# Modulation loads in buffers of their own, table loads and padding behind the first h, and half-contraction first feed-forward rounds in a hybrid decoder layer

## The chip, the cores and the metric

The kernel runs on 1 core of one Trainium2 chip. The metric is the device time of one execution in microseconds; three runs of the kernel before have a median of 1298.05 us (1289.34 to 1298.52).

## The reference

One decoder layer on x (256 tokens, 2048 features, float32), with a conditioning vector c. Six modulation vectors of 2048 come out of c; attention (8 heads) and a state-space branch (S5 and a gated linear unit) share one input and one output projection; a squared-ReLU feed-forward of 8192 follows.

```python
mod = (jax.nn.silu(c) @ w_ada + b_ada)[:, None, :]
sh1, sc1, g1, sh2, sc2, g2 = jnp.split(mod, N_MOD, axis=-1)

h = rms_norm(x, norm1_g) * (1.0 + sc1) + sh1
proj = h @ w_in
q, k, v, u = jnp.split(proj, [ATTN_WIDTH, 2 * ATTN_WIDTH, 3 * ATTN_WIDTH], axis=-1)
q = rms_norm(q.reshape(bsz, s, N_HEADS, HEAD_DIM), q_norm_g)
k = rms_norm(k.reshape(bsz, s, N_HEADS, HEAD_DIM), k_norm_g)
attn = dilated_attention(q, k, v).reshape(bsz, s, ATTN_WIDTH)

y = jax.nn.gelu(s5_mixer(u, lam_re, lam_im, log_step, b_re, b_im, c_re, c_im, d_skip))
ssm = y * jax.nn.sigmoid(y @ w_glu + b_glu)
mixed = jnp.concatenate([rms_norm(attn, attn_out_g), rms_norm(ssm, ssm_out_g)], axis=-1) @ w_out
x = x + g1 * mixed

h2 = rms_norm(x, norm2_g) * (1.0 + sc2) + sh2
ff = jnp.square(jax.nn.relu(h2 @ w_ff1)) @ w_ff2
return x + g2 * ff
```

## The kernel before, in words

**Products.** Activations lie feature-major, 256 tokens in the free dimension. Every large product is made of three reduced-precision products: a float32 value is split into a rounded part and a rest (`split`: ScalarE copies the rounded part, line 161, VectorE subtracts, line 136), for weights (`wh`, `wl`) and activations alike, and TensorE adds high by high, high by low and low by high. All weights come from memory in loads of 512 KB into `raw`, a pool of five buffers, and each is split once.

**Modulation.** `w_ada` is 96 MB in 24 blocks of four "pieces" of 1 MB. Blocks in PE_BLOCKS (8 of them) are multiplied on TensorE against a padded c (`cpad`, line 249, 2 to 4 short matmuls a load), the others on VectorE, which multiplies and sums along the row against a broadcast c (`cbc`, line 158, one instruction of 1024 columns per 512 KB). `pump(n)` takes the next n pieces, in the order ADA_ORDER; `pump_at(i)` takes PUMPS[i] of one. Where a piece is loaded is `ring["tags"]`, set from RINGS by stage: `raw`, the same pool as the weights (two halves of 512 KB), or a buffer that is unused just then (U, T0, PD, WB0). The first `h` group needs 8 pieces, the second 16, the third 24, the fourth 32; the output projection 48; the group kg of `h2`, the input of the feed-forward, 56 + 8 kg; the last ones are due at the end.

**Stages.** After c is padded and the tables of the state-space branch are loaded (`bb`, `cc`, `ident`), `make_h(0..3)` makes the normalised input in four groups of 512 features. The input projection (lines 193 to 195) interleaves with that, block by block over its 8 blocks of 512 output columns, u first; it is evicted into U, V and QK. Between its blocks stand the preparation of the state-space tables (`pad_write`, `toep_half`: copies on ScalarE, small matmuls), the state (`state_in`) and its scan, VectorE steps over the state H in XT. Then come the norms of q and k, `y_block` (lines 686 and 690, 32 steps of small matmuls on the finished state), the gate of the linear unit (`w_glu`, lines 798 to 800), attention in four pairs of heads, and `branch_scale`, which norms a branch and splits it. The output projection takes the state-space half first (8 `w_out_pair` of two 512 KB loads, called pairs of rounds here), then the attention half. `make_h2` and the feed-forward follow: 128 loads for `ff1`, 128 for `ff2`.

**A pair.** `pair_part` takes one 512 KB load of weights, makes 8 matmuls of 512 columns (line 848: the split activation's two parts side by side) and 8 of 256 (line 850) into two accumulator banks; the two halves of a bank are added on the way out. A pair works through 16 matmuls this way.

**Order.** The framework's scheduler decides at build how each engine's instructions are ordered, and every engine then works in that order. SyncE (SP) issues all loads, so a load that waits for its buffer holds up those behind it.

## Time and profile before

| | |
|---|---|
| median of three runs | 1298.05 us |
| profiled execution | 1299.06 us, of which span 1297.3 |
| mean granted TensorE clock | 0.946 of full |
| TensorE busy | 1198.6 us (92%), 6818 matmuls |
| VectorE busy | 921.8 us (71%) |
| ScalarE busy | 582.0 us (45%) |
| moved by DMA | 299.59 MB, 231 GB/s |

Engines: PE is TensorE's matmuls, PEld its weight loads, DVE VectorE, ACT ScalarE, SP SyncE. L848 is line 848 of the kernel before. An instruction is written output<-inputs, with a width, and a bracket behind it says how long its engine stood idle just before and what released it. The clock is a share of the full 2.4 GHz. Matmul durations overlap, so the distance from one start to the next is what a matmul costs in a full queue.

### The profile page before, as it was taken

How to read it: one execution, taken by the hardware profiler on the slowest of the kernel's cores; microseconds unless marked ns; L12 is line 12 of the kernel's file. 1: busy time of each engine (PE TensorE's matmuls, PEld its weight loads, DVE VectorE, ACT ScalarE, POOL GpSimd, SP SyncE). 2: the span in 40 equal slices, each digit the busy share in tenths (PEclk: the TensorE clock that was granted, in tenths of full speed). 3: DMA queues.
4: the chain of work that ended last, by engine and by line, in shares of the span. 5: the costliest groups of instructions: out<-in, count | busy, mean ns of one | idle time of the engine just before them, and what ended most of it. 6: DMA issues, size and time to landing. Idle time of an engine off the chain costs nothing.

```text
span 1297.3 us, 17972 instructions
## 1 busy us (share of the span) xinstructions
PE 1198.6 (92%) x6818; PEld 993.7 (77%) x6818; DVE 921.8 (71%) x1520; ACT 582.0 (45%) x807; POOL 13.0 (1%) x12
## 2 busy tenths in 40 slices
PE   5777999998987977949999999999999999999998
PEld 1355778865677866838888888888888888888887
DVE  9687678899555898877865556765566666667764
ACT  3579544322275533324544444443344443344432
POOL 3000000000000000000000000000000000000000
PEclk9788999999688897969999999999999999999999
DMA  9687898888544486748766666765677666667763
GB/s 345 228 271 259 337 341 314 286 313 289 196 149 162 149 302 213 255 154 275 242 220 188 189 217 224 248 192 184 190 233 239 224 183 191 205 235 248 241 211 96
DMA packets 82166, 299.59 MB, mean 231 GB/s; under 512 B 9120, under 2 KB 11424, under 8 KB 80288
## 3 DMA queue, kind: packets, MB, share of 16 engines
q1 hardware_dynamic: 82080, 298.45, 69.2%
q8 instruction: 53, 0.87, 0.3%
q14 instruction: 33, 0.27, 0.1%
HBM read 296.31 MB, written 2.10 MB: 230 GB/s over the span
## 4 chain that ended last, share of the span: by engine, by line
PE 76%; DVE 8%; DMA 7%; ACT 6%; issue 2%; SPq 0%; DVEq 0%; ACTq 0%
PE acc L848 37%; PE acc L850 18%; DMA raw<-w_ada 6%; PE acc L194 4%; PE acc L195 4%; PE acc L193 4%; DVE wl L136 2%; PE tr L249 2%; DVE raw L158 2%; PE acc L690 1%; ACT wh L161 1%; PE tr L553 1%; PE acc L686 1%; ACT TO L161 1%; PE tr L848 1%
## 5 line engine op out<-in xcount | busy, mean ns | idle before, releaser
L136 DVE TENSOR_TENSOR wl<-raw,wh 128x1024 fp32r<-128x1024 f32 x360 | 439.8, 1223 | 260.6 <-ACT wh L161 259.6
L161 ACT ACTIVATE wh<-raw 128x1024 fp32r<-128x1024 f32 x360 | 381.3, 1060 | 505.5 <-PE acc L848 347.2
L158 DVE SCALAR_TENSOR_TENSOR raw<-raw,cbc 128x1024 f32<-128x1024 f32 x112 | 136.6, 1222 | 53.7 <-DMA raw<-w_ada 53.1
L848 PE MATMUL acc<-CA,wh 128*128 128x512 f32 x608 | 167.0, 397 | 2.5 <-DVE XT L156 2.0
L848 PE MATMUL acc<-TO,wh 128*128 128x512 f32 x480 | 132.0, 396 | 0.6 <-DVE rows L136 0.6
L848 PE MATMUL acc<-QK,wh 128*128 128x512 f32 x384 | 107.4, 402 | 13.1 <-DVE QK L136 13.1
L848 PEld LDWEIGHTS acc<-CA,wh 128*128 128x128 f32 x608 | 104.7, 189 | 16.7 <-issue 2.2
L850 PEld LDWEIGHTS acc<-CA,wl 128*128 128x128 f32 x608 | 92.4, 188 | 13.1
L850 PE MATMUL acc<-CA,wl 128*128 128x256 f32 x608 | 96.1, 281 | 0.0
L848 PEld LDWEIGHTS acc<-TO,wh 128*128 128x128 f32 x480 | 82.5, 189 | 11.7 <-PE acc L850 0.8
L848 PEld LDWEIGHTS acc<-QK,wh 128*128 128x128 f32 x384 | 67.4, 193 | 22.4 <-issue 13.3
L850 PEld LDWEIGHTS acc<-TO,wl 128*128 128x128 f32 x480 | 73.3, 188 | 10.6
L850 PE MATMUL acc<-TO,wl 128*128 128x256 f32 x480 | 76.1, 281 | 0.0
L848 PE MATMUL acc<-WB,wh 128*128 128x512 f32 x256 | 69.8, 394 | 0.0
L850 PEld LDWEIGHTS acc<-QK,wl 128*128 128x128 f32 x384 | 58.3, 189 | 7.7
L850 PE MATMUL acc<-QK,wl 128*128 128x256 f32 x384 | 60.3, 279 | 0.0
L193 PE MATMUL acc<-wh,HA 128*128 128x512 f32 x128 | 48.6, 411 | 9.0 <-ACT wh L161 8.9
L194 PE MATMUL acc<-wl,HA 128*128 128x512 f32 x128 | 52.2, 408 | 0.0
L194 PE MATMUL acc<-wl,HB 128*128 128x512 f32 x128 | 50.7, 397 | 0.4 <-DVE wl L136 0.4
L195 PE MATMUL acc<-wh,HA 128*128 128x512 f32 x128 | 50.6, 401 | 0.0
L195 PE MATMUL acc<-wh,HB 128*128 128x512 f32 x128 | 50.0, 393 | 0.0
L848 PEld LDWEIGHTS acc<-WB,wh 128*128 128x128 f32 x256 | 43.7, 188 | 5.6
(269 smaller groups left out, 1763.5 us busy)
## 6 DMA issues: line engine op xcount, KB each, us to landing
raw<-w_ff SPq DMA_DIRECT2D x256, 512.0 KB, 4.3
raw<-w_ada SPq DMA_DIRECT2D x158, 512.0 KB, 5.2
raw<-w_in SPq DMA_DIRECT2D x64, 512.0 KB, 5.9
raw<-w_out SPq DMA_DIRECT2D x32, 512.0 KB, 4.8
U<-w_ada SPq DMA_DIRECT2D x8, 1024.0 KB, 7.3
XT<-xT SPq DMA_DIRECT2D x8, 512.0 KB, 5.8
T<-w_ada SPq DMA_DIRECT2D x8, 512.0 KB, 6.5
raw<-w_glu SPq DMA_DIRECT2D x8, 512.0 KB, 6.0
```

What stands on the lines that cost most here:

```text
L136: return (eng or self.nc.vector).tensor_tensor(out, a, b, op=op)
L158: self.nc.vector.scalar_tensor_tensor(out, a, s, b, op0=op0, op1=op1, accum_out=accum)
L161: self.nc.scalar.activation(out, a, AF.Copy, scale=scale)
L193: mm(ps, xh, wh, start=start, stop=False)
L194: mm(ps, xh, wl, start=False, stop=False)
L195: mm(ps, xl, wh, start=False, stop=stop)
L249: mm(acc[32 * q : 32 * q + 32, :], cpad[:, 4 * g + q, :], raw[:, i, :], start=g == 0, stop=g == 3,)
L553: mm(pv[:, r - r2, ri], wb[r // 8][:, r % 8, ri], u2[:, :, r, :], start=True, stop=True)
L686: mm(pv[:, r - r8], toep[:, r].rearrange("p g s j -> p (g s j)"), u2[:, :, r, :], start=True, stop=False)
L690: mm(pv[pr, r - r8], ca[pr, r, ri].rearrange("p s j -> p (s j)"), H[pr, ri, r, :], start=False, stop=ri == 1,)
L848: mm(pp[e], hi[:, e, kk], xs[kk].rearrange("p s n -> p (s n)"), start=first and kk == 0, stop=False)
L850: mm(pp[e][:, 0:SEQ], lo[:, e, kk], xs[kk][:, 0], start=False, stop=last and kk == 3)
```

## The change

**Loads.** RINGS and PUMPS change. The first pieces go to three buffers of 1 MB (Q, K, U; `QK` becomes two tensors, Q and K), in one load each, then Q and K alternate; `raw` and the old mixed rings come in the middle; from the norm of q and k on, pieces go to HA alone, from the gate on to HA and PD, one load of 1 MB each; from the feed-forward on to `raw`. The loads of `bb` and `cc` come after five pieces, `cbc` and `ident` after `h(0)`.

**Order at the start.** The sigmoids of c and the padding copies may be issued only after the last ScalarE instruction of `h(0)` (`issue_after(h_act)`).

**Pairs.** `pair_bank` replaces `pair_part` in the output projection and in the first rounds of the feed-forward: 24 matmuls of 256 columns into one bank, so that one eviction takes it.

**Modulation in the output projection** goes to 64 pieces instead of 80.

**First rounds of the feed-forward.** Before, 4 output groups ran through all four groups kg of `h2` at once, as `h2` came. Now 16 output groups run through kg 0 and 1 in two halves of 8 banks, their partial sums are copied to buffers, and kg 2 and 3 follow in `ff1`, which adds the partial sum. During the first 8 groups half a piece per load is taken, to 80.

```diff
-RINGS = (('raw',), ('raw',), ('T0', 'PD', 'raw', 'raw'), ('T0', 'raw', 'raw'), ('U', 'raw'), ('WB0', 'U', 'raw', 'raw'))
-PUMPS = (2.5, 2.75, 1.0, 1.5, 0.75, 0.75, 1.5, 1.25, 1.0, 2.0, 0.25, 2.75, 1, 0.75)
+RINGS = (('Q', 'K', 'U'), ('Q', 'K'), ('raw',), ('T0', 'PD', 'raw', 'raw'), ('T0', 'raw', 'raw'), ('raw',), ('HA',), ('HA', 'PD'))
+PUMPS = (2.0, 2.0, 1.0, 1.0, 1.0, 1.0, 1.0, 1.0, 1.0, 1.0, 1.0, 2.0, 1.0, 0.5)
...
     s5_small()
-    pump(8)
+    pump(5)
+    for w in range(2):
+        nc.sync.dma_start(bpow[w][:, 3], I["bb"][:, w])
+    nc.sync.dma_start(c0, I["cc"])
+    pump(3)
     h_end = make_h(0)
-    ring["tags"] = RINGS[0]
+    h_act = k.last_act
+    ring["tags"] = RINGS[1]
...
+    run(w_in_block(0, [0]), 0)
     nc.sync.dma_start(cbc, I["cbc"])
+    nc.sync.dma_start(idents, I["consts"][:, 0 : P + 32])
...
-        nc.scalar.activation(sg, cbc[:, sl], AF.Sigmoid)
+        with tc.issue_after(h_act):
+            nc.scalar.activation(sg, cbc[:, sl], AF.Sigmoid)
...
-    run(w_in_block(0, [0]), 0)
-    for w in range(2):
-        pad_write(lambda gp: padB[:, 16 * w : 16 * w + 16, :, gp, :], by_r(bpow[w][:, 0]))
+    with tc.issue_after(h_act):
+        for w in range(2):
+            pad_write(lambda gp: padB[:, 16 * w : 16 * w + 16, :, gp, :], by_r(bpow[w][:, 0]))
...
+    def pair_bank(bank, src, xs, first, last):
+        hi, lo = load_p(src)
+        for e in range(2):
+            o = bank[:, SEQ * e : SEQ * e + SEQ]
+            for kk in range(4):
+                mm(o, hi[:, e, kk], xs[kk][:, 0], start=first and e + kk == 0, stop=False)
+                mm(o, hi[:, e, kk], xs[kk][:, 1], start=False, stop=False)
+            for kk in range(4):
+                mm(o, lo[:, e, kk], xs[kk][:, 0], start=False, stop=last and e + kk == 4)
...
-            pump_at(12, 80)
+            pump_at(12, 64)
...
+    def ff1_half(base):
+        banks = [tr() for _ in range(4)] + [k.acc() for _ in range(4)]
+        for kg in range(2):
+            if base == 0:
+                make_h2(kg)
+            for i in range(8):
+                pair_bank(banks[i], I["w_ff1"][base + i, kg], h2[4 * kg : 4 * kg + 4], kg == 0, kg == 1)
+                pump_at(13, 80)
+        for i in range(8):
+            copy(part[base + i], banks[i])
...
-    ff1_first()
-    for np_ in range(4, 8):
+    ff1_half(0)
+    ff1_half(8)
+    make_h2(2)
+    make_h2(3)
+    for np_ in range(8):
         ff1(np_)
```

**The order of the loads at the start.** On SyncE, right behind the first small load and the four of x, the kernel before issues these (raw is the pool of five, the number a counter):

```order
L212 DMA WB_3_68<-bb 128x512
L212 DMA WB_4_69<-bb 128x512
L215 DMA ident_72<-consts 128x160
L217 DMA T_6_74<-cc 128x1024
L178 DMA raw_245<-w_ada 128x1024
L178 DMA raw_247<-w_ada 128x1024
L178 DMA raw_253<-w_ada 128x1024
L178 DMA raw_255<-w_ada 128x1024
L178 DMA raw_261<-w_ada 128x1024
L600 DMA cbc_76<-cbc 128x2048
L178 DMA raw_263<-w_ada 128x1024
```

Behind it come eleven more halves of the first 8 pieces and then the first weights of the input projection.

The kernel after, SyncE from the same place:

```order
L233 DMA K_241<-w_ada 128x2048
L233 DMA U_247<-w_ada 128x2048
L233 DMA Q_253<-w_ada 128x2048
L585 DMA WB_3_68<-bb 128x512
L585 DMA WB_4_69<-bb 128x512
L586 DMA T_6_71<-cc 128x1024
L178 DMA raw_350<-w_in 128x1024
L178 DMA raw_356<-w_in 128x1024
L597 DMA cbc_72<-cbc 128x2048
L598 DMA ident_70<-consts 128x160
```

Three whole pieces now stand ahead of the tables, and `cbc` and `ident` behind the first two loads of the input projection's weights.

SyncE, the rows right behind those:

```order
L178 DMA raw_482<-w_in 128x1024
L178 DMA raw_488<-w_in 128x1024
L178 DMA raw_600<-w_in 128x1024
L233 DMA K_259<-w_ada 128x2048
L233 DMA U_274<-w_ada 128x2048
L233 DMA Q_283<-w_ada 128x2048
L178 DMA raw_606<-w_in 128x1024
L178 DMA raw_648<-w_in 128x1024
L178 DMA raw_654<-w_in 128x1024
L233 DMA K_289<-w_ada 128x2048
L233 DMA U_295<-w_ada 128x2048
```

K_289 is the 7th piece and U_295 the 8th; ahead of K_289 stand the 6th, 7th and 8th load into the pool of five, which need three of its buffers back.

**The matmuls ahead of y.** On TensorE, from the last matmuls of the input projection to the first finished step of y (line 249: a modulation piece; 686 and 690: y), in the kernel before:

```order
L194 MATMUL acc_2454<-wl_2464,HB_1710 128x512
L195 MATMUL acc_2454<-wh_2463,HB_1710 128x512
L249 MATMUL tr_2491<-raw_2492,cpad_81 32x512 x2
L249 MATMUL tr_2491<-raw_2494,cpad_81 32x512 x2
L249 MATMUL tr_2491<-raw_2546,cpad_81 32x512 x2
L249 MATMUL tr_2491<-raw_2548,cpad_81 32x512 x2
L249 MATMUL tr_2491<-raw_2554,cpad_81 32x512 x2
L686 MATMUL acc_2562<-PD_1831,TO_155 128x64
L686 MATMUL acc_2625<-PD_1831,TO_155 128x64
L686 MATMUL acc_2683<-PD_1831,TO_155 128x64
L690 MATMUL acc_2562<-XT_1834,CA_162 64x64 x4
L686 MATMUL acc_2562<-PD_1831,TO_155 128x64
```

The rows of y that read the state (line 690) stand here behind five halves of pieces, all in the pool of five.

The same place on TensorE in the kernel after (line 245 is the old 249, 256 the old 260, HA the single buffer):

```order
L245 MATMUL tr_2270<-raw_2413,cpad_77 32x512 x2
L686 MATMUL acc_2480<-PD_1769,TO_151 128x64
L686 MATMUL acc_2528<-PD_1769,TO_151 128x64
L686 MATMUL acc_2576<-PD_1769,TO_151 128x64
L686 MATMUL acc_2632<-PD_1769,TO_151 128x64
L256 MATMUL tr_2421<-ones_73,rows_2419 128x1 x4
L245 MATMUL tr_2473<-HA_2474,cpad_77 32x512 x4
L245 MATMUL tr_2473<-HA_2522,cpad_77 32x512 x4
L245 MATMUL tr_2473<-HA_2570,cpad_77 32x512 x4
L245 MATMUL tr_2473<-HA_2618,cpad_77 32x512 x4
L690 MATMUL acc_2480<-XT_1772,CA_158 64x64 x4
L686 MATMUL acc_2480<-PD_1769,TO_151 128x64
```

Four pieces that pass through one buffer, each a load that may go out only when the matmuls of the one before are done, now stand between the first matmuls of y and the rest.

**VectorE between the gate and the branch's norm.** In the kernel before (line 158: a modulation product; products into `WB_502` are the gate; the last row begins the norm, `rs`):

```order
L158 SCALAR_TENSOR_TENSOR raw_3537,adap_2739<-raw_3537,cbc_76 128x1024
L136 TENSOR_TENSOR T_494_2785<-T_494_2785 128x512
L136 TENSOR_TENSOR WB_502_2825<-rows_3193,WB_502_2825 128x256
L136 TENSOR_TENSOR WB_502_2825<-rows_3197,WB_502_2825 128x256
L158 SCALAR_TENSOR_TENSOR raw_3544,adap_3543<-raw_3544,cbc_76 128x1024
L158 SCALAR_TENSOR_TENSOR raw_3546,adap_3543<-raw_3546,cbc_76 128x1024
L136 TENSOR_TENSOR adap_2739<-adap_2739 128x1
L136 TENSOR_TENSOR adap_3543<-adap_3543 128x1
L136 TENSOR_TENSOR mod_84<-adap_2739,small_61 128x4
L152 TENSOR_SCALAR rs_2545<-tr_3255 128x2
```

Of the modulation's instructions there are three products here and their sums.

The same stretch on VectorE in the kernel after:

```order
L156 SCALAR_TENSOR_TENSOR HB_2470<-HB_2470 128x384
L136 TENSOR_TENSOR WB_468_2714<-rows_3108,WB_468_2714 128x256
L136 TENSOR_TENSOR WB_468_2714<-rows_3112,WB_468_2714 128x256
L156 SCALAR_TENSOR_TENSOR HB_2470<-HB_2470 128x384
L725 RECIPROCAL den_3132<-den_3132 128x2
L150 TENSOR_SCALAR WB_446_2469<-WB_446_2469,den_3132 128x128
L150 TENSOR_SCALAR WB_446_2469<-WB_446_2469,den_3132 128x256
L725 RECIPROCAL den_3144<-den_3144 128x2
L150 TENSOR_SCALAR WB_446_2469<-WB_446_2469,den_3144 128x128
L150 TENSOR_SCALAR WB_446_2469<-WB_446_2469,den_3144 128x256
L136 TENSOR_TENSOR T_460_2674<-T_460_2674 128x512
L152 TENSOR_SCALAR rs_2472<-tr_3170 128x2
```

It holds attention's rows and the gate's last product, and no modulation.

## Rows read from the trace of the kernel before

**Rows 1.** The page's first line: the span and all instructions.

```profile
span 1297.3 us, 17972 instructions
```

**Rows 2.** Windows by stage: stretch, us, busy PE, PEld, DVE, ACT, POOL, PEclk, DMA, GB/s.

```profile
59.40:140.00 80.60, 64.18 (x332) 49.00 (x332) 64.81 (x119) 66.54 (x127) 1.82 (x1) 0.87 0.80 271
140.00:311.10 171.10, 170.08 (x844) 129.21 (x845) 144.87 (x210) 66.86 (x82) 0.22 (x1) 1.00 0.87 315
311.10:360.90 49.80, 47.10 (x402) 31.05 (x402) 29.54 (x51) 11.44 (x17) 0.00 (x0) 0.70 0.65 226
360.90:428.30 67.40, 54.51 (x343) 50.48 (x343) 42.96 (x114) 43.58 (x89) 0.00 (x0) 0.80 0.42 141
428.30:482.30 54.00, 51.09 (x292) 44.29 (x290) 46.58 (x95) 21.72 (x32) 0.00 (x0) 0.99 0.73 240
...
495.40:549.40 54.00, 52.87 (x306) 46.51 (x306) 42.49 (x76) 19.96 (x22) 0.00 (x0) 0.95 0.69 233
549.40:573.40 24.00, 3.97 (x20) 3.50 (x20) 19.07 (x46) 6.73 (x15) 0.00 (x0) 0.57 0.69 238
573.40:662.00 88.60, 87.97 (x491) 76.43 (x492) 68.89 (x104) 41.87 (x56) 0.00 (x0) 0.98 0.68 227
662.00:1297.30 635.30, 631.36 (x3606) 551.44 (x3604) 402.16 (x521) 272.21 (x314) 0.00 (x0) 1.00 0.66 207
```

**Rows 3.** Timeline, TensorE: start, us, instruction, idle before it and who ended it.

```profile
495.37 2.04 PE L848 MATMUL acc<-QK,wh 128*128 128x512 f32 x4 [13.08 <-DVE QK L136]
```

**Rows 4.** Timeline, TensorE: products of 256 in the gate, and halves of old pairs.

```profile
380.12 0.28 PE L798 MATMUL acc<-TO,wh 128*128 128x256 f32 x1
380.24 0.28 PE L799 MATMUL acc<-TO,wh 128*128 128x256 f32 x1
...
640.28 1.09 PE L848 MATMUL acc<-CA,wh 128*128 128x512 f32 x4
...
641.68 1.10 PE L848 MATMUL acc<-CA,wh 128*128 128x512 f32 x4
```

**Rows 5.** Timeline: the padding copies on ScalarE, and the first projection matmul.

```profile
53.57 3.40 ACT L161 ACTIVATE WB<-CA 64x768 f32<-64x768 f32 x4
...
59.43 0.50 PE L193 MATMUL acc<-wh,HA 128*128 128x512 f32 x1
```

**Rows 6.** Timeline, VectorE: steps of the scan, sums of squares, scaling of q and k.

```profile
309.06 1.04 DVE L136 TENSOR_TENSOR XT<-XT,T 128x480 f32<-128x480 f32 x1
...
310.01 0.68 DVE L660 TENSOR_REDUCE qss<-rows 128x4 f32<-128x512 f32 x1
310.60 1.25 DVE L136 TENSOR_TENSOR T<-XT,apow 128x496 f32<-128x496 f32 x2
...
337.57 3.50 DVE L136 TENSOR_TENSOR QK<-QK,qss 128x1024 f32<-128x1024 f32 x3
```

**Rows 7.** Timeline, TensorE: two steps of y early and two late.

```profile
314.57 0.45 PE L690 MATMUL acc<-XT,CA 64*64 64x64 f32 x8
...
315.31 0.45 PE L690 MATMUL acc<-XT,CA 64*64 64x64 f32 x8
...
322.36 0.69 PE L690 MATMUL acc<-XT,CA 64*64 64x64 f32 x8
...
323.60 0.69 PE L690 MATMUL acc<-XT,CA 64*64 64x64 f32 x8
```

**Rows 8.** The page's DMA issues: a whole piece, KB, us from issue to landing.

```profile
U<-w_ada SPq DMA_DIRECT2D x8, 1024.0 KB, 7.3
```

**Rows 9.** Timeline, VectorE: a modulation product between gate and norm.

```profile
407.10 1.22 DVE L158 SCALAR_TENSOR_TENSOR raw<-raw,cbc 128x1024 f32<-128x1024 f32 x1 [1.46 <-DMA raw<-w_ada]
```

**Rows 10.** Windows in the output projection, 10 us each, columns as in rows 2.

```profile
450.00:460.00 10.00, 10.00 (x61) 8.80 (x60) 8.04 (x16) 5.61 (x6) 0.00 (x0) 1.00 0.92 327
470.00:480.00 10.00, 9.63 (x53) 8.41 (x54) 10.00 (x21) 2.12 (x2) 0.00 (x0) 1.00 0.87 273
```

**Rows 11.** Timeline, VectorE: a modulation product ahead of the feed-forward.

```profile
564.99 1.23 DVE L158 SCALAR_TENSOR_TENSOR raw<-raw,cbc 128x1024 f32<-128x1024 f32 x1 [1.89 <-DMA raw<-w_ada]
```

More of the change, by code (lines that the diff above doesn't have):

```diff
@@ L160, in copy @@
     def copy(self, out, a, scale=1.0):
-        self.nc.scalar.activation(out, a, AF.Copy, scale=scale)
+        self.last_act = self.nc.scalar.activation(out, a, AF.Copy, scale=scale).ins
     def rsqrt(self, out, v, tmp, tmp2):
@@ L336, in w_in_evict @@
         if c not in accs:
-            if c in "uv":
-                accs[c] = t(c.upper(), [P, 2, AW])
-            else:
-                if "qk" not in accs:
-                    accs["qk"] = t("QK", [P, 2, 2, AW])
-                accs[c] = accs["qk"][:, "qk".index(c)]
+            accs[c] = t(c.upper(), [P, 2, AW])
         for m in range(2):
@@ L823, in branch_scale @@
         row_bcast(rb, rs[:, 0, o : o + 2])
-        b = t(tag, [P, 8, 2, SEQ], F32R)
+        b = [t(tag, [P, 8 // len(tags), 2, SEQ], F32R) for tag in tags]
+        b = [w[:, c] for w in b for c in range(8 // len(tags))]
         for c in range(8):
             stt(v[:, c], v[:, c], g[:, c : c + 1], rb, ALU.mult, ALU.mult)
-            k.split(b[:, c, 0], b[:, c, 1], v[:, c])
+            k.split(b[c][:, 0], b[c][:, 1], v[:, c])
         return b
-    xss = branch_scale("CA", yg, col["sog"], sq2, 2)
+    xss = branch_scale(("CA",), yg, col["sog"], sq2, 2)
     pump(99, until=48)
@@ L850, in pair_part @@
                 mm(pp[e][:, 0:SEQ], lo[:, e, kk], xs[kk][:, 0], start=False, stop=last and kk == 3)
+    def pair_bank(bank, src, xs, first, last):
[7 more added lines that the diff above has]
+                mm(o, lo[:, e, kk], xs[kk][:, 0], start=False, stop=last and e + kk == 4)
     def w_out_pair(half, x8, np_):
-        pp = [k.acc(), k.acc()]
+        bank = k.acc()
         for kg in range(2):
-            xs = [x8[:, 4 * kg + kk] for kk in range(4)]
-            pair_part(pp, I["w_out"][np_, 2 * half + kg], xs, kg == 0, kg == 1)
+            xs = x8[4 * kg : 4 * kg + 4]
+            pair_bank(bank, I["w_out"][np_, 2 * half + kg], xs, kg == 0, kg == 1)
         for e in range(2):
             c = 2 * np_ + e
-            for s in (1, 0):
-                stt(
-                    z[:, c], pp[e][:, SEQ * s : SEQ * s + SEQ], mod[:, 32 + c : 33 + c], z[:, c], ALU.mult, ALU.add
-                )
+            stt(z[:, c], bank[:, SEQ * e : SEQ * e + SEQ], mod[:, 32 + c : 33 + c], z[:, c], ALU.mult, ALU.add)
     for np_ in range(8):
@@ L903, in make_h2 @@
         for c in range(4 * kg, 4 * kg + 4):
-            v = nsq[c // 8][:, c % 8]
+            if c % 2 == 0:
+                vv = t("rows", [P, 2, SEQ], bufs=2)
+            v = vv[:, c % 2]
             stt(v, z[:, c], g2c[:, c : c + 1], r2, ALU.mult, ALU.mult)
@@ L966, in ff2 @@
                 nc.sync.dma_start(out[c], y)
-    ff1_first()
-    for np_ in range(4, 8):
+    ff1_half(0)
[3 more added lines that the diff above has]
+    for np_ in range(8):
         ff1(np_)
+    y2 = [t("WB2", [P, 8, SEQ]), t("WB3", [P, 8, SEQ])]
+    y2 = [y2[c // 8][:, c % 8] for c in range(16)]
     for G in range(4):
```

79 lines of the change are left out of this document (34 added, 45 removed).

## The prediction

> **What bounds the kernel now.** I read first the span [rows 1], then the windows, cut where one stage gives way to the next [rows 2], then the timeline at the cuts. The windows show two kernels in one. From 662 us on TensorE is busy 631.4 of 635.3 us at the full clock (2.4 GHz) and the loads need 207 GB/s: bound by matmuls alone. Before 662 it is the same in one stretch only (140 to 311.1, 170.1 of 171.1). Elsewhere something is lost: from 59.4 to 140 TensorE works 64.2 of 80.6 us while ScalarE works 66.5; from 311.1 to 360.9 it is busy but at a mean clock of 0.70; from 482.3 it stands still until 495.4, waiting for the attention branch that VectorE scales [rows 3]; from 549.4 to 573.4 it works 4.0 of 24.0 us. Only in such stretches can the change win, and it can lose anywhere. The profiled execution took 1299.06 us (span and 1.8 us around it), 1.0 above the median of the three runs; sums go against 1299.06 and 1.0 comes off at the end.
>
> **The matmuls.** A pair of the old kind (half the k-tiles 512 wide, half 256) shows two halves starting 1.40 us apart, so 2.80 a pair; three products of 256 columns, as the projection of the gate already does them, start 0.12 us apart [rows 4], so 24 of them take 2.86. Sixty-four pairs change kind: about 4 us more, contained in the stretches below. The 224 pairs behind stay: 0 for the last 635 us. The second of the new steps there, a VectorE add in place of a ScalarE copy, lies under a VectorE that is busy 402 of 635 us [rows 2]; without that cover it would be 32 short instructions.
>
> **The first h and what follows it: -8.** Now the first projection matmul starts at 59.43, and 53.57 to 56.97 of the path is four padding copies on ScalarE [rows 5]. Those copies, and the sigmoids of c, are queued behind h, and three modulation pieces go out before the tables. Against that, SP waits for three weight splits before it may issue the 7th piece (first piece of order above). I take the first matmul at about 55: -4. The copies are not saved, only moved into a stretch where ScalarE has 14 us to spare of 80.6; but three weight splits instead of two now run before h, and the second h's inputs no longer wait behind six padding copies: another -4. Ends: 0 (the ScalarE queue eats all) and -14 (all its idle time goes).
>
> **To the end of the input projection: -6.** Pieces whose matmuls TensorE does before that end: 24.5 before, 20 after, by the two orders. 4.5 pieces at about 1 us and one block's transposes less, in a stretch where TensorE is the bound. Ends: 0 and -8.
>
> **Scan and y: +10.** Here the change costs. In the order of after, VectorE's queue behind the last eviction of the projection holds eight reductions (0.68), four scalings of q and k (3.50 for three), three wide scan steps and the first group of the last one (1.25 and two more adds, 2.6) [rows 6]; the wide ones I put at 3.8, and with a split and small ones that is 28 us before y may read its first group. Before, that group was ready 3 us after the projection. Then y's 32 steps need 0.74 us each at the full clock and 1.24 at the half level [rows 7]: 24 to 40 us; I take the middle, 32. So 60 us where the stretch has 49.8: +10. Ends: +2 (24 us) and +18 (40 us). The four one-buffer pieces that TensorE takes one after the other ahead of y (second piece of order) cost three round trips of 7.3 us [rows 8] and a matmul group of about 1: 25 us, hidden under those 28. Which clock y gets: in the old stretch it was 0.70 although TensorE was busy 47.1 of 49.8 us [rows 2]. The Trainium skill, page "TensorE: Matmul & The Clock Gate", section "What's actually happening", has the full clock as what sustained activity earns; by that, y would take 24 us and the sum would be 8 us lower. The rows show a busy engine staying low, so I do not count on it.
>
> **Gate and branch scaling: -7.** In the 67.4 us from 360.9, six modulation products of 1.22 us stand in VectorE's queue between the gate and the norm, one of them after a wait of 1.46 us for its load [rows 9]: 9 us, and in the new order none is there (third piece). TensorE now takes four pieces from single buffers in this stretch; I give back 2. Ends: -9 and +8 (one whole wait of 8.3).
>
> **Output projection, first half: -9.** 428.3 to 495.4 is 67.1 us. The 13.1 us of standing go if the attention branch is scaled in time: in the new order no modulation product stands ahead of it on VectorE, and its scaling stands before the 12th weight split of 16. What is left is 54.0 plus four pieces that TensorE now does here, 4. Ends: -13 and 0.
>
> **Second half: -2.** 54.0 us now. It has 16 pairs and some 8 pieces to load, 8.4 + 8.4 MB. The matmuls take 46 us; at 327 GB/s, the rate of the nearest stretch, in which loads of both kinds run beside a full TensorE [rows 10], the loads take 51. I take 52. Ends: -8 and (at 273) +8. One accumulator bank and two evictions fewer per pair are hidden: VectorE is busy 42 of 54 us.
>
> **The gap to the feed-forward: -10.** Of 24.0 us, seven modulation products and waits for their loads (such as 1.89 us [rows 11]) stand on VectorE's queue along the chain from the last eviction to h2. The new order keeps two. Five products and 4 us of waits go. Ends: -13 and 0.
>
> **First 32 pairs of the feed-forward: +14.** What was not loaded before must be loaded here: 16 pieces beside 32 weight loads, 33.6 MB, where 88.6 us at 227 GB/s moved 20. TensorE would need 91 us, the loads at 327 GB/s 103. VectorE has 16 pieces at 2.4 and 32 splits at 1.2, under 90, so it does not bind. The copies of 16 banks on ScalarE (busy 42 of 88.6) are hidden. Ends: +3 and (at 273) +34.
>
> **Sum.** -8 -6 +10 -7 -9 -2 -10 +14 = -18: 1281, so 1280 as a median.
>
> **Rivals.** (a) *The loads keep up.* Then the feed-forward start costs 3 instead of 14, the second half gains 8 instead of 2, and y runs mostly at the full clock, +3: -18 -11 -6 -7 = -42, 1256. For it: the demand, 365 GB/s, is only a tenth over what was moved at 450. Against: five shared buffers and a full VectorE queue. (b) *Nothing is gained, the wait moves.* At 273 GB/s the two loading stretches come to +8 and +34 in place of -2 and +14: +12 in sum, 1310; with the gap gaining all 13 it is 1306. For it: from 470 to 480 VectorE was full and the loads got 273 [rows 10]. Against: VectorE carries less in these stretches than there. (c) *Slower: TensorE stands in line behind one buffer.* Twelve pieces for TensorE pass through the single buffers HA and PD, in its queue in program order. A wait that nothing hides is 7.3 + 1.0 = 8.3 us; four lie under the scan and one quarter of one is in the sum. Of the other eight, three exposed eat the gain (18 + 2 over 8.3) and four make it slower by over 1%; with five it is 1280 + 40 = 1320. For it: a wait of that sort, at 13 us, is the only long one TensorE has in its own queue [rows 3]. Against: most of these loads are issued long before their matmuls. The Trainium skill, page "TensorE: Matmul & The Clock Gate", section "HAM oscillation — how this bites in real kernels", says that matmul bursts with a load's wait between them start at the low clock each time, which would add to (c); the low stretch at y is of that kind.
>
> **How the numbers follow.** The forecast with its own range 1266 to 1294: 0.42. (a) 0.27, (b) 0.14, (c) 0.17. A time within 1%, which is about what a measurement of this kernel can tell from none, is 1285 to 1311. Of the forecast's 0.42 I put 0.25 below 1285 and 0.17 within; (a) is all faster; (b) is 0.11 within and 0.03 slower; (c) is slower. That is 0.52, 0.28, 0.20. The range of 1250 to 1312 takes in (a) and (b) and leaves out most of (c) and the far end of (a).
>
> **What would show it.** First projection matmul near 55; end of that projection near 297; y ending near 357; TensorE not standing between the halves of the output projection; a gap of about 14 us before the feed-forward; about 103 us for its first 32 pairs, with the loads at over 300 GB/s; 635 us for the rest. I am wrong if the loads hold TensorE up at y or in the gate, if the last stretch moves, or if y starts soon after the projection.

## The result, and the profile after

The changed kernel takes 1309.99 us (median of four runs, 1308.36 to 1311.06); the kernel before took 1294.62 beside it (1289.34 to 1298.52). The ratio is 1.012, interval 1.0073 to 1.0167: slower by 1.2%, where 1280 was forecast. The profiled execution has a span of 1309.2 us against 1297.3 [rows 1]: +11.9, where the sum said -18.

```profile
span 1309.2 us, 18900 instructions
```

The windows of the changed kernel, cut at the same events as [rows 2] (stretch, us, busy PE, PEld, DVE, ACT, POOL with their counts, PEclk, DMA share, GB/s):

```profile
59.00:140.00 81.00, 68.08 (x425) 53.47 (x423) 58.28 (x91) 75.85 (x142) 1.82 (x1) 0.93 0.67 230
140.00:312.50 172.50, 165.19 (x766) 123.22 (x766) 137.89 (x211) 62.75 (x76) 0.22 (x1) 0.99 0.82 287
312.50:339.70 27.20, 9.62 (x55) 2.73 (x54) 26.98 (x46) 7.90 (x12) 0.00 (x0) 0.64 0.59 212
339.70:378.40 38.70, 38.70 (x325) 31.84 (x322) 7.31 (x12) 2.39 (x4) 0.00 (x0) 0.50 0.08 28
378.40:439.70 61.30, 53.88 (x369) 47.48 (x369) 31.68 (x83) 42.27 (x83) 0.00 (x0) 0.84 0.54 189
439.70:498.70 59.00, 58.11 (x473) 53.81 (x474) 43.95 (x88) 30.82 (x52) 0.00 (x0) 1.00 0.63 213
498.70:551.10 52.40, 52.40 (x442) 52.20 (x440) 40.87 (x54) 21.28 (x24) 0.00 (x0) 1.00 0.78 282
551.10:564.30 13.20, 2.92 (x12) 2.57 (x12) 8.95 (x22) 2.03 (x5) 0.00 (x0) 0.67 0.69 234
564.30:670.60 106.30, 96.98 (x768) 95.24 (x768) 79.91 (x130) 44.21 (x58) 0.00 (x0) 0.96 0.80 273
670.60:1309.20 638.60, 631.23 (x3584) 550.32 (x3584) 431.31 (x598) 271.23 (x307) 0.00 (x0) 1.00 0.67 210
```

Set against the forecast, stage by stage (the lengths are the differences of the cuts; "again" is a second profile of each kernel, taken side by side, below):

| stage | forecast | first profiles | again |
|---|---|---|---|
| to the first projection matmul | -4 | 59.4 to 59.0: -0.4 | 59.3 to 60.4: +1.1 |
| to the end of the projection | -4 -6 | 251.7 to 253.5: +1.8 | 249.0 to 247.7: -1.3 |
| scan and y | +10 | 49.8 to 65.9: +16.1 | 50.8 to 66.1: +15.3 |
| gate and branch scaling | -7 | 67.4 to 61.3: -6.1 | 64.9 to 61.3: -3.6 |
| output projection, first half | -9 | 67.1 to 59.0: -8.1 | 68.1 to 60.9: -7.2 |
| second half and gap | -2 -10 | 78.0 to 65.6: -12.4 | 76.2 to 65.9: -10.3 |
| first 32 feed-forward pairs | +14 | 88.6 to 106.3: +17.7 | 88.9 to 106.6: +17.7 |
| the other 224 pairs | 0 | 635.3 to 638.6: +3.3 | 635.2 to 637.6: +2.4 |

In the second profile of the changed kernel one matmul of the output projection stands 4.7 us ahead of the others, so the gate and the first half are best read together there (-10.8, and -14.2 in the first profiles).

The gains in the middle came. The whole gain at the start (14 us) did not, scan and y cost 6 more than forecast, the feed-forward 7 more.

### The profile page after: what moved, and what is told of

Read it like the earlier page. It is cut to its first block, busy times and chain, and to the rows that moved or that the text cites. A ratio compares the mean times of both kernels' runs of the same rounds, so it can differ in the third digit from the quotient of the medians.

```text
span 1309.2 us, 18900 instructions
## 1 busy us (share of the span) xinstructions
PE 1209.6 (92%) x7330; PEld 1022.6 (78%) x7330; DVE 916.8 (70%) x1493; ACT 578.2 (44%) x792; POOL 13.0 (1%) x12
## 3 DMA queue, kind: packets, MB, share of 16 engines
q1 hardware_dynamic: 78336, 298.45, 68.1%
## 4 chain that ended last, share of the span: by engine, by line
PE 70%; DMA 13%; DVE 9%; ACT 6%; issue 2%; SPq 0%; ACTq 0%; DVEq 0%
PE acc L849 31%; PE acc L851 16%; DMA raw<-w_ada 9%; PE acc L859 2%; PE acc L858 2%; PE acc L861 2%; DVE raw L158 2%; DVE wl L136 2%; PE tr L245 2%; PE acc L194 2%; PE acc L690 1%; PE acc L195 1%; PE acc L686 1%; PE acc L193 1%; DMA HA<-w_ada 1%
## 5 line engine op out<-in xcount | busy, mean ns | idle before, releaser
L158 DVE SCALAR_TENSOR_TENSOR raw<-raw,cbc 128x1024 f32<-128x1024 f32 x94 | 114.6, 1223 | 48.0 <-DMA raw<-w_ada 46.9
L849 PE MATMUL acc<-CA,wh 128*128 128x512 f32 x512 | 139.7, 398 | 7.1 <-DVE rows L136 3.8
L849 PEld LDWEIGHTS acc<-CA,wh 128*128 128x128 f32 x512 | 88.9, 189 | 20.2 <-ACT wh L161 5.2
L851 PE MATMUL acc<-CA,wl 128*128 128x256 f32 x512 | 80.6, 283 | 0.0
L849 PE MATMUL acc<-TO,wh 128*128 128x512 f32 x256 | 70.3, 396 | 0.0
L195 PE MATMUL acc<-wh,HB 128*128 128x512 f32 x128 | 50.0, 399 | 0.0
L193 PE MATMUL acc<-wh,HB 128*128 128x512 f32 x128 | 47.4, 405 | 2.7 <-DVE V L136 1.6
L849 PEld LDWEIGHTS acc<-TO,wh 128*128 128x128 f32 x256 | 43.8, 188 | 5.7
L851 PEld LDWEIGHTS acc<-WB,wl 128*128 128x128 f32 x256 | 39.2, 188 | 5.6
L851 PEld LDWEIGHTS acc<-TO,wl 128*128 128x128 f32 x256 | 39.1, 188 | 5.7
L851 PE MATMUL acc<-WB,wl 128*128 128x256 f32 x256 | 40.8, 281 | 0.0
L851 PE MATMUL acc<-TO,wl 128*128 128x256 f32 x256 | 40.6, 280 | 0.0
L194 PEld LDWEIGHTS acc<-wl,HB 128*128 128x128 f32 x128 | 24.5, 191 | 14.6 <-DVE wl L136 4.6
```

The source lines that it names most:

```text
L158: self.nc.vector.scalar_tensor_tensor(out, a, s, b, op0=op0, op1=op1, accum_out=accum)
L193: mm(ps, xh, wh, start=start, stop=False)
L194: mm(ps, xh, wl, start=False, stop=False)
L195: mm(ps, xl, wh, start=False, stop=stop)
L849: mm(pp[e], hi[:, e, kk], xs[kk].rearrange("p s n -> p (s n)"), start=first and kk == 0, stop=False)
L851: mm(pp[e][:, 0:SEQ], lo[:, e, kk], xs[kk][:, 0], start=False, stop=last and kk == 3)
```

## The experiments

All stage times below are differences of TensorE's events in one profile each, so a few us of the projection's length (247.7 to 253.5 for the changed kernel itself) are scatter.

### The two kernels once more

> The changed kernel once more, as the profile to set the others of this call against: 1310, with the projection's stretch at 249 to 254 us (three variants with the same order there took 248.3 to 250.2, the first profile 253.6).

> The kernel before once more, on the chip of this call: 1297, each stage within 1 us of its first profile but the projection, where TensorE waits on loads, within 4.

Measured: 1308.2 and 1294.3, stages in the table above. The projection of before came 2.7 us under its first length, the rest within 2.5.

### y: VectorE's queue, the one buffer, and the clock

The changed kernel, VectorE ahead of y (start, us, instruction):

```profile
333.77 2.35 DVE L136 TENSOR_TENSOR Q<-Q,qss 128x1024 f32<-128x1024 f32 x2
336.04 2.35 DVE L136 TENSOR_TENSOR K<-K,qss 128x1024 f32<-128x1024 f32 x2
338.31 0.67 DVE L136 TENSOR_TENSOR XT<-XT,T 128x496 f32<-128x496 f32 x1
```

and TensorE at the same place:

```profile
337.81 1.94 PE L245 MATMUL tr<-HA,cpad 128*32 128x512 f32 x8 [4.95 <-DMA HA<-w_ada]
339.68 0.69 PE L690 MATMUL acc<-XT,CA 64*64 64x64 f32 x8
...
340.92 0.69 PE L690 MATMUL acc<-XT,CA 64*64 64x64 f32 x8
```

The scaling of q and k stands ahead of the scan's last add (the row into XT), and the fourth piece through HA ends 0.77 us after that add: two causes that end within a microsecond of each other. From 339.68 the steps of y are 1.24 us apart.

```diff
-... ('raw',), ('HA',), ('HA', 'PD'))
+... ('raw',), ('raw',), ('HA', 'PD'))        # y_raw
```

> The changed kernel, with the modulation pieces between the norm of q and k and the gate taken through the pool of five (raw) again instead of the one buffer HA. In the changed kernel TensorE starts the state part of y at 339.7, 27.2 us behind the projection's end; its last HA piece ends at 339.75 and VectorE's first finished group of the scan at 338.98. Theory V (VectorE's queue: reductions and scalings of q and k stand ahead of the scan's last steps): y starts within 1 us of the same place, 26 to 27 us behind the projection, and the time stays at 1309 within 3. Rival H (four loads through one buffer, each waiting for the matmuls before): without the three round trips y starts 10 us or more sooner and the time falls to 1299.

Measured: y starts 22.7 us behind the projection, the time is 1297.5. The window of this kernel from the projection's end to y:

```profile
307.80:330.50 22.70, 12.34 (x61) 4.20 (x61) 21.33 (x36) 10.29 (x15) 0.00 (x0) 0.74 0.82 280
```

Neither theory has its number. TensorE's last work ahead of y ends at 324.7 and it then waits 5.9 us for VectorE, busy 21.33 of 22.70: without HA, VectorE still holds y up. The 4.7 us that were won (27.4 in the changed kernel's second profile) are as long as the scalings of q and k (2.35 and 2.35), which the scheduler now puts behind the first finished group. The span is 10.7 us shorter than in that profile: besides the 4.7, y takes 36.7 in place of 38.7, and 5 fell in the output projection and the feed-forward, which this edit does not explain.

```diff
+        with tc.issue_after(scan_end):         # y_scan
             nc.vector.reduce_sum(
```

> The changed kernel, with the eight reductions of q and k (and so the root and the four scalings) held behind the last step of the scan in VectorE's queue. HA stays. Theory V: 8 x 0.68 + 4 x 1.17 + about 1 us of small ones, 11 us, go from ahead of the first finished group; y starts about 16 us behind the projection, and the time is 1298; y itself keeps 1.2 us a step, since it starts behind a stall as before. Rival H: y starts 25 us or more behind the projection still, and the time stays at 1309.

Measured: 19.0 us behind the projection, 1302.6. The windows of this kernel:

```profile
310.60:329.60 19.00, 5.79 (x37) 2.33 (x37) 16.96 (x25) 2.74 (x4) 0.00 (x0) 0.64 0.68 247
329.60:372.00 42.40, 42.40 (x337) 32.22 (x337) 18.82 (x31) 7.38 (x12) 0.00 (x0) 0.50 0.14 51
```

8.2 of theory V's 11 us came. But the scheduler also moved two of the four HA pieces into y (at 2 us each at the half clock, so y is 3.7 longer), and with them two of the three round trips. So this run alone does not tell the two causes apart. best_cold (below) has both edits, and there y starts 14.1 us behind the projection: y_raw took 4.7 us off 27.4, y_scan 8.4, both together 13.3. The pool of one buffer and VectorE's queue each held y up. In all three kernels, the changed one, y_raw and y_scan, y runs at 0.50 from its first to its last step, with TensorE idle for 0.02 us at most.

```diff
+        if hp == 0:                            # y_warm, ahead of y_block(0)
+            kw = tr()
+            for i in range(110):
+                mm(kw, hs[3][:, 0, 0, 0:P], hs[3][:, 0, 0:2].rearrange("p a n -> p (a n)"), start=True, stop=True)
```

> The changed kernel with 110 extra matmuls of 512 columns that nobody reads, put on TensorE between the first HA piece and y, about 26 us at the full clock, so that TensorE does not stand there. Theory C (a stall ahead of y is what costs the clock, and y holds the clock that it starts with): y's 32 steps take 0.74 us each, about 26 us with three pieces among them, and the time is 1309 - 12 = 1297. Rival D (y's small matmuls cannot hold the full clock whatever stands ahead of them, as in the kernel before, where the clock fell to half 8 us into y): y starts at 0.74 a step and goes to 1.24 after 8 to 10 us, 34 us in all, and the time is 1305.

Measured: 1299.4. Windows: the extra work, y, and the gate with the branch's scaling:

```profile
311.00:340.00 29.00, 29.00 (x140) 22.70 (x140) 28.90 (x48) 8.01 (x12) 0.00 (x0) 1.00 0.31 113
340.00:365.20 25.20, 25.20 (x338) 18.70 (x337) 5.46 (x10) 2.39 (x4) 0.00 (x0) 1.00 0.34 110
365.20:432.20 67.00, 56.91 (x376) 50.22 (x376) 31.86 (x84) 42.38 (x83) 0.00 (x0) 0.82 0.51 185
```

Theory C: y holds the full clock for all of its 25.2 us, 13.5 less than at the half clock; rival D's fall 8 to 10 us into y did not come. But 5.7 come back in the gate (67.0 against 61.3).

The kernel before shows where its own clock fell. TensorE in its second profile, from the third step of y on:

```profile
313.24 0.45 PE L690 MATMUL acc<-XT,CA 64*64 64x64 f32 x8
...
317.43 1.92 PE L249 MATMUL tr<-raw,cpad 128*32 128x512 f32 x4 [3.12 <-DMA raw<-w_ada]
...
320.52 0.69 PE L690 MATMUL acc<-XT,CA 64*64 64x64 f32 x8
```

One load of a modulation piece comes 3.12 us late (2.7 in the first profile); the steps ahead of it take 0.74 us, those behind it 1.24. In b_pair (below), whose instructions stand in the same order on every engine until well behind y, the same load came 0.45 us late and the clock stayed there:

```profile
316.20 1.05 PE L249 MATMUL tr<-raw,cpad 128*32 128x512 f32 x4 [0.45 <-DMA raw<-w_ada]
...
317.92 0.45 PE L690 MATMUL acc<-XT,CA 64*64 64x64 f32 x8
```

It did not stay to the end of y. Windows of b_pair, where y ends at 346.7:

```profile
330.00:340.00 10.00, 10.00 (x130) 6.88 (x120) 7.97 (x8) 3.19 (x4) 0.00 (x0) 1.00 0.97 329
340.00:346.70 6.70, 6.70 (x58) 5.56 (x58) 2.21 (x7) 0.00 (x1) 0.00 (x0) 0.59 0.68 249
```

TensorE is busy throughout, so a wait is not the only thing that costs the level; what took it here stays open.

The last test covers that wait in the kernel before, with the edit of y_warm and 24 matmuls.

> The kernel before with 24 extra matmuls of 512 columns ahead of y on TensorE (5.6 us at the full clock), whose result nobody reads. In both profiles of before, TensorE waits 2.7 and 3.1 us for one modulation load in the third step of y, and the granted clock is 0.50 from there on for 20 us and more; y takes 46.3 and 47.3 us. In the kernel before with one bank in the output projection that load came 0.4 us late, the clock stayed at 1.00 for 27 us, and y took 33.5. Theory C (it is the stall that costs the clock, and y at the half clock cannot raise it): the extra work covers the wait, y takes 33 us, and the time falls by 13 - 6 + 3 = 10 us to about 1280, a ratio of 0.992. Rival X (the clock's fall is not tied to this wait): y stays at 46 us and the time rises by the 5.6 us to 1296 or more.

Measured: 1295.8, ratio 1.0048 (1.0017 to 1.0079), slower by half a percent. Windows of y and of the gate:

```profile
319.90:351.30 31.40, 31.40 (x376) 22.82 (x375) 20.08 (x34) 6.75 (x10) 0.00 (x0) 0.97 0.74 262
351.30:422.70 71.40, 55.70 (x345) 51.41 (x343) 43.12 (x114) 46.46 (x91) 0.00 (x0) 0.79 0.41 135
```

The mechanism is as in theory C: no wait, the clock at 0.97, y 15.9 us shorter than in before_again. The time is not. Counted from the projection's end, y starts 6.2 later and the gate takes 71.4 in place of 64.9, so the output projection begins 3.2 us sooner only. In the gate TensorE waits 15.1 us in place of 11.4, most of it for ScalarE, and is busy 2.5 us longer.

So y's saving came to nearly nothing here, but it need not: in b_pair y was 13.8 us shorter than in before_again, the gate took 65.6 (to where the output projection's matmuls follow one another), and the span was 11.4 us shorter. The extra matmuls of b_dense also led the scheduler to another order on the other engines around y; whether that, or the shorter y, made the gate longer was not tested. Why the median is 7 us above that of before beside it, while the profiles lie 0.5 us apart, stays open; before itself ranged there from 1284 to 1302.

### The start

SyncE in the changed kernel (issue time, duration):

```profile
24.78 0.33 SPq L233 DMA_DIRECT2D Q<-w_ada  x1
34.45 5.14 SPq L178 DMA_DIRECT2D raw<-w_in  x3
39.69 0.37 SPq L233 DMA_DIRECT2D K<-w_ada  x1
40.17 0.37 SPq L233 DMA_DIRECT2D U<-w_ada  x1
```

After the 6th piece, SyncE stands from 25.1 to 39.6 but for the issue of three weight loads, each of which waits for a buffer that a weight split must free first, and the 7th and 8th pieces go out behind them.

```diff
-    run(w_in_block(0, [0]), 0)
+    with tc.issue_after(p8):                   # start_hold; also blocks 1, 6 and 7
+        run(w_in_block(0, [0]), 0)
```

> The changed kernel, with the first eight loads of the projection's weights held behind the 8th modulation piece in SyncE's queue. In the changed kernel SyncE stands from 25.1 to 39.7 with the 7th piece behind weight loads that wait for their buffers, and the 8th goes out at 40.2; first projection matmul at 58.96. Theory Q (SyncE's queue stood in line behind weight splits): the 8th piece goes out near 34, h is ready near 51, the first projection matmul starts at 51 to 53, and the end comes 5 to 8 us sooner, 1302. Rival B (three buffers and their round trips set the pace): the 8th still goes out at 39 or later, since its buffer comes free at 39.1, and the time changes by less than 2 us. A second rival: the weights now come late, and what is won before the first matmul is lost in the first blocks.

Measured: 1323.1. The 8th piece goes out at 33.7, the first projection matmul starts at 52.6, both as theory Q has it; the projection then takes 273.4 us. 6.4 us are won ahead of the first matmul and 20 or more lost behind it, as the second rival has it. Its reason, weights that come late, is not what the trace shows: from 52 to 140 us none of ScalarE, VectorE and TensorE waits for a weight load.

```profile
52.60:80.00 27.40, 22.86 (x158) 14.89 (x158) 14.62 (x26) 26.75 (x49) 0.00 (x0) 0.87 0.51 186
```

ScalarE is busy 26.75 of the first 27.4 us there, and 58.44 of the 64.1 us to the first matmul on the second h, at 116.7. In the changed kernel that matmul comes at the same 116.7: what was won is gone by then, and 13 us more are lost after it, which the edit does not explain. ScalarE is as full in the first 20 us of the changed kernel and of the kernel before it, in this order:

```profile
59.00:80.00 21.00, 19.84 (x145) 13.95 (x142) 8.88 (x14) 20.51 (x34) 0.00 (x0) 0.96 0.54 183
```

```profile
59.40:80.00 20.60, 15.38 (x74) 9.74 (x77) 16.46 (x30) 19.53 (x36) 0.00 (x0) 0.87 0.79 268
```

The 14 us that ScalarE had to spare lie behind these 20. In the changed kernel TensorE stands 6.2 us, up to 86.0, for one copy on ScalarE that has 17 others right ahead of it in its queue (its waits in the projection, in total, times, longest):

```profile
PE tr L256 <- ACT rows L161: 6.2, 1, 6.2
```

```diff
-        with tc.issue_after(h_act):            # s_pad; all three places
-            nc.scalar.activation(sg, cbc[:, sl], AF.Sigmoid)
+        nc.scalar.activation(sg, cbc[:, sl], AF.Sigmoid)
```

> The changed kernel with the sigmoids of c and the padding copies not held behind the first h on ScalarE (the three places of issue_after(h_act) taken out); the rest of the start as changed. Forecast put 4 us on taking the copies from ahead of h, since ScalarE had 14 us to spare behind it. Theory S (they are only moved, into a stretch where ScalarE is full: 20.55 of the 21.04 us behind the first projection matmul): the first projection matmul comes up to 4 us later than 59.0 to 60.4, the projection ends within 2 us of the changed kernel's (308 to 312) and the time is 1308 within 3. Rival: holding them is worth its 4 us, and the projection ends at 314 or later.

Measured: 1320.0; first matmul at 62.0, the projection's end at 324.7. Theory S falls, the rival holds: with these loads, letting the copies go first costs 2 to 3 us ahead of the first matmul and 9 to 15 behind it. By the first matmul on the second h (120.9, in place of 116.7 and 115.5) 4 to 5 us are lost, so the hold is worth its 4 us. The rest comes later, where TensorE waits for VectorE's weight rests (8.2 us in the projection) and ScalarE. The edit lets the scheduler order all engines anew, so the 12 us are those of one other order, not of the copies alone.

> The kernel before with the start of the change alone: Q and K as two tensors, the first pieces in K, Q and U, the tables' loads and the copies behind the first h, in the changed kernel's order; from the second h on everything as before. The forecast had 4 us for the first h and 4 for what follows; the changed kernel twice gave the first projection matmul at 59.0 and 60.4 against 59.4 and 59.3, and the projection's end at 312.5 and 308.1 against 311.1 and 308.3. Theory N (the start gains nothing: SyncE stands behind weight splits until 39.7, and the copies land where ScalarE is full): first matmul at 58.5 to 60.5, second h within 3 us of the 119 of before, projection's end 307 to 312. Rival G (the start gains its 8, and the changed kernel loses them again later in the projection, by its other rings and paces): the projection ends at 304 or sooner.

Measured: first matmul at 58.6, the first matmul on the second h at 115.8 (119.5 and 118.6 in before, 116.7 and 115.5 in the changed kernel), the projection's end at 305.0, the time 1289.0 beside 1288.4 for before. Between the two theories: -3.3 to -6.1 at the projection's end, of which up to 4 may be scatter. The start alone gains some 3 us of the forecast 8 by the second h. The changed kernel has that gain there too, and does not keep it.

### The output projection

> The kernel before with one part of the change alone: the output projection takes three products of 256 columns into one bank with one eviction (pair_bank) in place of 512 and 256 into two banks with two. In the changed kernel the output projection with its standing took 8 us less, and the gap behind it 12 us less. Theory P (it is the modulation pieces that went elsewhere, evictions and banks were hidden): the two halves stay at 52 to 55 us each, TensorE still stands 12 to 14 us between them, the gap stays at 24 to 25, and the time is 1295 within 3. Rival E (fewer evictions on VectorE): the standing or the gap shrinks by 4 us or more, and the time is 1290 or less.

Measured: the halves 63.5 (with the standing, now 9.5) and 60.9, the gap 24.3; the time 1282.9. The windows of this kernel:

```profile
407.50:471.00 63.50, 57.62 (x432) 55.29 (x432) 53.98 (x118) 28.54 (x49) 0.00 (x0) 0.93 0.63 217
471.00:531.90 60.90, 55.87 (x440) 54.65 (x440) 43.82 (x73) 22.55 (x25) 0.00 (x0) 0.95 0.77 260
531.90:556.20 24.30, 2.29 (x13) 1.90 (x12) 16.03 (x41) 6.03 (x15) 0.00 (x0) 0.57 0.65 214
```

Theory P for the part itself. Both halves together take 124.4 where before takes 119.8 and 120.0, but a first matmul stands 4.7 us ahead of the rest; without it they take 119.7. The gap does not move. One bank does not bring the gains of this stretch; that leaves the pieces that the change loads elsewhere, which no run moved by themselves. The 1282.9 goes with a y that is mostly at the full clock (33.5 us in place of 47), behind the load above that came only 0.45 us late, and is no result of the edit.

### The first feed-forward rounds

```diff
-                pump_at(13, 80)                # ff_skip
+    for b in ADA_ORDER[16:20]:
+        nc.vector.memset(mod[:, 4 * b : 4 * b + 4], 0.0)
+    state["left"] -= 16
```

> The changed kernel with the 16 modulation pieces beside the first feed-forward rounds left out (four blocks of the modulation are zero). The first 32 pairs took 106.3 us, against 88.6 before. Theory L (48 MB-halves share five buffers, and the loads bind): without the pieces the 32 pairs take 90 to 93 us, as 32 pairs of 2.86 need, and the time is 1295. Rival M (the half contraction itself stalls TensorE: banks, copies of partial sums, the inputs of kg 1): they take over 100 us still. The stretch behind, the first 45 us of which lost 3.3 us, should get them back under L.

Measured: 1289.4. The 32 pairs take 94.7 us and the gap 6.5:

```profile
553.50:648.20 94.70, 94.67 (x768) 94.37 (x769) 52.54 (x68) 46.44 (x62) 0.00 (x0) 0.97 0.58 178
```

Theory L, with its size 2 us off: TensorE is full, so 94.7 is what these matmuls need, and the pieces cost 11.6 us here and 6.7 in the gap. The last stretch still takes 639.5, where before takes 635.3: that loss isn't theirs. In it the changed kernel waits 7.2 us, 3.4 of them once for a weight split and the rest here (total, times, longest):

```profile
PE acc L849 <- DVE rows L136: 3.8, 2, 2.3
```

The rows tile is the add of the partial sum: for 16 output groups, of which 8 follow one another at the head of this stretch, a pair of banks now carries two loads in place of four, so its eviction must keep up at twice the rate.

```diff
-    ring["tags"] = ("raw",)
+    ring["tags"] = ("HA", "U", "Q", "K")       # ff_bufs, to the end of ff1_half(8)
```

> The changed kernel, with the 16 modulation pieces of the first feed-forward rounds loaded whole into four buffers that are idle there (HA, U, Q, K), so that the pool of five is left to the weights. Nothing is left out. Leaving the pieces out took the gap ahead of the feed-forward from 13.2 to 6.5 us and the 32 pairs from 106.3 to 94.8. Theory L5 (the five shared buffers bind, not what memory can deliver): the 32 pairs take 95 to 98 us, the gap 8 to 11, the time 1297. Rival R (memory's rate binds, 33.6 MB at about 320 GB/s): the 32 pairs take 103 us or more and the time stays above 1305.

Measured: 1298.4; gap 9.9, 32 pairs 96.3:

```profile
551.10:561.00 9.90, 2.29 (x13) 1.90 (x12) 8.73 (x17) 2.10 (x5) 0.00 (x0) 0.70 1.02 419
561.00:657.30 96.30, 94.80 (x769) 93.89 (x770) 76.39 (x96) 46.27 (x62) 0.00 (x0) 0.98 0.77 268
```

Theory L5. Nothing is left out and TensorE is full: 13.3 of the 18 us that the pieces cost came back with buffers of their own. Memory's rate did not bind: ahead of the pairs the loads ran at 419 GB/s. The edit also loads a piece whole and gives VectorE fewer instructions for it (96 in place of 130 in the 32 pairs), and no run has this without the buffers. In the changed kernel ScalarE's splits waited for these in the 32 pairs:

```profile
ACT wh L161 <- DMA raw<-w_ff: 19.3, 10, 6.4
ACT wh L161 <- DVE raw L158: 17.5, 5, 5.9
```

The second row is a weight in line behind a modulation product for its turn. In ff_bufs neither is left, and what they wait for most is TensorE:

```profile
ACT wh L161 <- PE acc L859: 24.9, 16, 2.7
```

### The mends together

> The changed kernel with three mends together: pieces ahead of the gate through the pool of five (y_raw), the norm of q and k behind the scan on VectorE (y_scan), and the feed-forward's pieces in four idle buffers (ff_bufs). If the three add: y starts 17 to 19 us behind the projection in place of 27.3, takes 37 to 40 us at the half clock, gap and 32 pairs take 106 us together in place of 120: 1308 - 9 - 0 - 14 = 1285, a ratio of 0.992 to the kernel before. If y and the feed-forward do not add (a wait that comes back in the gate), 1292 or more.

> The same with 75 extra matmuls of 512 columns on TensorE ahead of y (18 us at the full clock), whose result nobody reads, so that y starts at the full clock. If y holds the clock that it starts with: y takes 25 to 27 us in place of 37 to 40, of which some 4 us come back as waits in the gate (as in y_warm, where the gate took 67.0 in place of 61.3): 1277, a ratio of 0.986. If y starts before the clock has risen or the extra matmuls hold y up, no better than the one without.

> The three mends together with 50 extra matmuls in place of 75 ahead of y (11.8 us at the full clock). Without any, y started 14.0 us behind the projection, its clock was 0.95, 1.00 and then 0.54, and the times lay between 1269 and 1291; with 75 y started 20.9 us behind, ran at 1.00, and the times lay between 1278 and 1285. Theory C: y starts 15 to 16 us behind the projection at the full clock and takes 25 to 28 us, and the time is 1273 with a small spread, a ratio of 0.987. Rival: the clock falls in some executions all the same, and median and spread are those without extra work.

Measured: 1278.7 without extra matmuls (ratio 0.9915, 0.9872 to 0.9958; 1269 to 1291), 1279.7 with 75 (0.9932, 0.9904 to 0.9961; 1278 to 1285), 1276.9 with 50 (0.9891, 0.9841 to 0.9941; 1274 to 1282). The mends add, and all three beat both kernels, the kernel before by about 1%. Without extra matmuls y took 28.7 us, not the 37 to 40 that were expected: the clock was at 0.95 to 1.00 from 323 to 340 us and at 0.54 from there on. The times with extra matmuls spread less; no gain in the median is shown. Windows of the one with 50, ahead of y, and y (its gap takes 9.9 us, its 32 pairs 95.3):

```profile
308.90:325.10 16.20, 16.20 (x84) 11.38 (x84) 15.42 (x22) 1.75 (x3) 0.00 (x0) 1.00 0.32 112
325.10:351.90 26.80, 26.80 (x343) 20.76 (x340) 20.14 (x31) 10.08 (x15) 0.00 (x0) 0.95 0.52 173
```

## Why the prediction was wrong, step by step

The sum was 30 us off: 15.4 at the start and in the projection, 6.1 in scan and y, 7 in the feed-forward, the rest within 1 to 2. The first of these alone takes the gain from 18 us to 3; the others make it a loss.

**The first h and what follows it (-8).** The step that failed is "I take the first matmul at about 55: -4". That matmul came at 59.0 and 60.4 (59.4 and 59.3 before). SyncE stood 14 us behind weight splits, which the text names against the term and then gives no price. start_hold shows that without this wait the matmul comes 6.4 us sooner, and also that these 6.4 are gone at the second h, behind a ScalarE that is full. The other -4 came for the most part: the second h's first matmul is at 116.7 and 115.5, in place of 119.5 and 118.6. "A stretch where ScalarE has 14 us to spare" is an average over 80.6 us and hid that ScalarE is full at its head (19.53 of 20.6); yet s_pad shows that the hold was worth its 4 us at the second h. What was won there was lost in the projection.

**The projection (-6).** The step that failed is "in a stretch where TensorE is the bound". From the first projection matmul to the end, the stretch went from 251.7 and 249.0 to 253.5 and 247.7, where -4 -6 was forecast. The count held: 78 piece matmul instructions in the stretch in place of 116. They took 15.5 us in place of 17.9, so the 4.5 pieces were worth 2.4 us. One half of the small padding products (64 matmuls, 2.4 us) moved from ahead of the first projection matmul into this stretch. And behind 140 us TensorE now stands 7.3 us (5.7 in the second profile) where it stood 1.0 (0.5), mostly for the weight rests that VectorE makes. Its waits for these in the projection, the kernel before and then the changed one (total, times, longest):

```profile
PE acc L194 <- DVE wl L136: 0.4, 1, 0.4
```

```profile
PE acc L194 <- DVE wl L136: 5.3, 5, 1.9
```

b_start, which has the old rings and paces behind the second h, stands 0.6 us there. So the loss goes with the new rings and paces and the order that they bring; which of them, and why the rests come late, was not tested.

**Scan and y (+10; +16).** 28 us ahead of y were forecast, 27.2 measured. HA's round trips were not quite hidden, though: the last piece ends 0.77 us after VectorE's add. The mis-sized term is y: 38.7 us for 32, since the middle between both clocks was taken. Two things in the trace of before pointed to the half clock: y's late steps [rows 7], and the load's wait ahead of them, which rival (c) speaks of and this term does not use. Against it stood the full clock of y's first steps, and those came straight out of the projection, without a stall.

**Gate, output projection, gap (-28; -21 to -27).** Right in sum, and for the output projection and the gap b_pair excludes the other cause, that one bank brought it. The second half hit its number by luck: its 52 us were to be those of loads at 327 GB/s over 46 us of matmuls, and TensorE was busy 52.40 of 52.40 us while the loads ran at 282.

**The first 32 pairs (+14; +17.7).** Right in that loads bind. The rate was 273 GB/s, the lower end, in place of 327. But the term goes by a rate, and ff_bufs shows that the five shared buffers bind (with what its edit changes beside them), not memory: with four more, the pairs took 96.3 us. The 91 us for the matmuls alone were 94.7.

**The rest (0; +3).** "A VectorE that is busy 402 of 635 us" is an average again. In the first 49 us of this stretch VectorE is busy 47.1, and the doubled rate of evictions there was not costed.

**Rivals.** (b), the gain turned into waits, was nearest in time (1310, or 1306, which its own terms make 1307) and was given 0.14. That is luck: the 273 GB/s of its feed-forward came, but its two terms, +8 and +34, came as -1.6 and +17.7, and nothing of it priced the start. (c) did not happen as priced: TensorE waits for HA three times, 17.6 us in all and all ahead of y, where VectorE's queue takes all but 0.77 us of the same time. No piece through HA or PD held it up later.

## What to carry to other kernels

Slack is a property of a moment: before work is moved to where an engine "has room", read that engine in windows as long as the moved work (here 20 us), not as long as the stage. A gain at one point of a stage is no gain at its end: 3 us at the second h were lost again within the projection. Where loads of two kinds share a small pool, count the buffers before the bytes: four idle buffers, with whole loads into them, brought back 13 of 18 us. And a short wait on TensorE ahead of many small matmuls can cost several times its own length in clock (3.1 us of wait, and y 13.8 us longer than with 0.45); yet look at what follows, since in y_warm and b_dense part or all of what y saved came back in the gate.

## What the runs showed of the hardware

A dense run of small matmuls did not raise TensorE's clock by itself. In the changed kernel y, nearly all matmuls of 64 columns, kept TensorE busy 38.70 of 38.70 us at a granted clock of 0.50 throughout (1.2 of 2.4 GHz); behind dense matmuls of 512 columns, in y_warm, it ran at 1.00 for 25.2 of 25.2 us. The Trainium skill, page "TensorE: Matmul & The Clock Gate", section "What's actually happening", says that activity releases the throttle; for these matmuls the trace disagrees, and the measurement decides.

A wait of 2.7 to 3.1 us stood where the full level was lost in the kernel before, and with one of 0.45 us in the same place it was kept. The Trainium skill, page "TensorE: Matmul & The Clock Gate", section "HAM oscillation — how this bites in real kernels", has a load's wait from which the next matmuls start at the low clock; here the trace agrees.

Inside y the level also changed without such a wait. It rose amid pieces of 512 columns (0.78 from 340 to 350 us in the kernel before). It fell under a busy TensorE: 0.59 from 340 us on in b_pair and 0.54 from 340 on in best_cold, each after 1.00. The longest wait ahead of these falls is 0.8 us, and what causes them stays open.
